# Order of the high and the low weight matmuls inside one product of a transformer layer's two projections

## The chip, the cores and the metric

The kernel runs on one core of one Trainium2 chip. The metric is the device time of one execution in microseconds (us). The same kernel was run three times; its median stands for it. A profile belongs to one further execution, whose own time is given beside it.

## The reference

The reference computes one decoder layer in float32 for a single sequence of 512 tokens with 2048 features. A first projection maps the input to 12288 columns: three groups of 1024 for a gated convolution, and queries, keys and values of three attention patterns of eight heads each. The convolution and the windowed attention follow, then an output projection, a residual and a layer norm. A second projection (up) maps to 2 x 5632 columns; a causal convolution of width 3, a gate and a down projection follow, and a second residual and layer norm. Cut to what matters here:

```
proj = x @ w_in                                # first projection: 512 x 2048 by 2048 x 12288
u, gate_b, gate_c, q, k, v = split(proj)
y_conv = gate_b * causal_conv3(gate_c * u, conv_w)
y_attn = dilated_window_attention(q, k, v, rel_bias)
x = layernorm(ALPHA * x + concat(y_conv, y_attn) @ w_out)
up = causal_conv3(x @ w_up, ffn_conv_w) + b    # second projection: 512 x 2048 by 2048 x 11264
a, g = split(up)
out = layernorm(ALPHA * x + (silu(g) * a) @ w_down)
```

## The kernel before, in words

**Splitting into high and low.** TensorE is used in a one-pass float32 form (`fp32r`) that keeps fewer bits of its operands. So every operand is split in two: a high part, rounded by a copy on ACT (L217 for weights, L312 for activations), and a low part, the rest, by a subtraction on DVE (L220 and L313). A product is then high x high + high x low + low x high. In the code `op.hi` and `op.lo` are the two parts of a weight block, `xh` and `xl` those of an activation block.

**Seven products instead of eight.** The two projections go by a scheme of Strassen's kind. The tokens, the features and the output columns are each halved. One output pair `p` (two blocks of 128 columns) is made of seven products of sums and differences of blocks instead of eight plain ones. `PROD` (L67) names for each product its activation block, its weight block and the region of PSUM in which it adds up; `MAIN` and `LAST` (L72, L73) are the orders in which the seven are run. A few pairs at the start of each projection are made otherwise: one by plain products (`PLAIN`), and five whose first two products are run ahead (`run_pre`, L378), while the activations still arrive. The first projection has 48 pairs, the second 44.

**One product.** A product sums over 1024 features, that is over eight steps `k` of 128. The weights are the stationary operand, a 128x128 block for each step, which is loaded anew for every matmul (the rows PEld of the profile). There are two forms of it.

- *Wide* (`product_wide`, L342). In each step a matmul with the high weights streams both parts of the activations side by side, 512 columns (L349), and a matmul with the low weights streams the high activations alone, 256 columns, into the second half of the same PSUM bank (L351). The two halves are added afterwards. That is 16 matmuls a product. `run_wide` (L414) uses it, for all regular pairs of the first projection and every third one of the second.
- *Narrow* (`product`, L362). In each step there are three matmuls of 256 columns into half a bank: high weights on high activations (L371), high weights on low activations (L372), low weights on high activations (L373). That is 24 matmuls a product. It is used for the pairs at the start of both projections and for two of three regular pairs of the second.

**What sets the order.** Each engine runs its instructions in the order in which the code issues them; the order is written out by hand (`manual_schedule`). `take` (L245) hands the next weight block over, after its low part has been issued on DVE; `free` (L254) gives its slot back and pumps further blocks: load by DMA on SP's queue (L182), the difference of two blocks on DVE where the scheme needs one (L207), high part on ACT, low part on DVE. There are four slots for high and four for low weights (`RING`, L60) and three for raw ones. After a product come the copies of its PSUM region (L446 for wide, L467 for narrow) and, some products later, the sums on DVE.

**The rest.** Attention (L767 to L872) is run with the output projection between its steps. The output and the down projection use a third form, `tm_unit` (L508 to L516): activations as the stationary operand, weights as the moving one, always 512 columns.

Of the kernel before, what the change touches and what calls it, by code (L numbers as in the profile page):

```python
# [18 lines left out]
P = 128  # L19
# [61 lines left out]
def _banks(q):  # L81
    return {"m" if PROD[i][2] in ("x1", "x2") else "n" for i in (q if isinstance(q, str) else [q])}
# [38 lines left out]
def layer_kernel(ctx: ExitStack, tc: tile.TileContext, xT, x, w_in, w_out, w_up, w_down, cw, fw, lnp, lnc, table,  # L121
# [3 lines left out]
    mm = nc.tensor.matmul  # L125
# [119 lines left out]
    def take():  # L245
        i = st["used"]
        if st["front"] <= i:
            pump()
        assert st["front"] > i
        back_upto(i + 1)  # L250
        st["used"] += 1
        return ops[i]
# [83 lines left out]
    def wide_region(p, name):  # L336
        rg = pairb.setdefault(p, {})
        if name not in rg:
            rg[name + "i"], rg[name] = get_bank()
        return rg[name]  # L340

    def product_wide(p, q, X, last):  # L342
        op = take()
        xn, _, reg = PROD[q]
        first = reg not in pairb.get(p, {})
        ps = wide_region(p, reg)
        for k in range(8):
            w = slice(k * P, (k + 1) * P)
            mm(ps, op.hi[:, w], X[xn].both(k), start=first and k == 0, stop=False,  # L349
               skip_group_check=True)  # L350
            mm(ps[:, 256:], op.lo[:, w], X[xn][0][:, k], start=False, stop=last and k == 7, skip_group_check=True)  # L351
        return op

    def region(p, name):
        rg = pairb.setdefault(p, {})
        b = "m" if name in ("x1", "x2") else "n"
        if b not in rg:
            rg[b + "i"], rg[b] = get_bank()
        return rg[b][:, 256:] if name in ("x1", "x3") else rg[b][:, :256]


    def product(p, q, X, last):  # L362
        op = take()
        for q in q if isinstance(q, str) else [q]:
            xn, _, reg = PROD[q]
            xh, xl = X[xn][0], X[xn][1]
            first = not _banks(q) & set(pairb.get(p, {}))
            ps = region(p, reg)
            for k in range(8):
                w = slice(k * P, (k + 1) * P)  # L370
                mm(ps, op.hi[:, w], xh[:, k], start=first and k == 0, stop=False, skip_group_check=True)  # L371
                mm(ps, op.hi[:, w], xl[:, k], start=False, stop=False, skip_group_check=True)  # L372
                mm(ps, op.lo[:, w], xh[:, k], start=False, stop=last and k == 7, skip_group_check=True)  # L373
        return op

# [2 lines left out]
    def run_pre(pl, X, keep, hook):  # L378
        pre = [(p, q) for p, seq, early in pl if early for q in seq]
        for i, (p, q) in enumerate(pre):  # L380
            free(product(p, q, X, False))
            if i == len(pre) - 4:
                for r in sorted({p for p, q in pre if q == "a"}):
                    kept[r] = keep()
                    for j, reg in enumerate(("x2", "x3")):
                        nc.scalar.activation(kept[r][:, j], region(r, reg), AF.Copy)
            hook()

    def run_plain(pl, X, otile, done, hook):
        def finish(p):  # L390
            o = otile()
            for i, reg in ((0, "x2"), (2, "x3")):
                nc.scalar.activation(o[:, i], region(p, reg), AF.Copy)
            for i, j, reg in ((1, 0, "x4"), (3, 1, "x1")):
                nc.vector.tensor_add(o[:, i], region(p, reg), kept[p][:, j])
            free_banks.extend((pairb[p]["ni"], pairb[p]["mi"]))
            del pairb[p]
            done(p, o)

        for p, seq, pre in pl:  # L400
            if pre or not _plain(seq):
                continue
            for i, q in enumerate(seq):
                op = product(p, q, X, not _banks(q) & set().union(*map(_banks, seq[i + 1:])))
                if i == len(seq) - 1:
                    later(2, functools.partial(finish, p))
                free(op)
                tick()
                hook()
# [4 lines left out]
    def run_wide(p, seq, X, stile, otile, put_block, done, hook):  # L414
# [26 lines left out]
        for i, q in enumerate(seq):  # L441
            left = set(seq[i + 1:])
            op = product_wide(p, q, X, PROD[q][2] not in {PROD[j][2] for j in left})
            if q in (1, 5, 6):
                sn[q] = stile(str(q))
                nc.scalar.activation(sn[q], pairb[p][PROD[q][2]], AF.Copy)  # L446
            for block, need in WNEED.items():
                if block not in sent and not need & left:
                    sent.add(block)
                    later(2, functools.partial(combine, block))  # L450
            free(op)
            tick()
            if hook:
                hook(p, q)

    def run_pairs(pl, X, stile, otile, bands, done, hook=None, put_block=None, every=1):
        for p, seq, pre in pl:
# [26 lines left out]
            for i, q in enumerate(seq):  # L484
                left = set(seq[i + 1:])
                op = product(p, q, X, not _banks(q) & set().union(*map(_banks, left)))
                if q in SNAP:
                    snap(q)
                for b, need in (("m", {7, 2, 5}), ("n", {3, 4, 6, 7})):
                    if b not in sent and not need & left:  # L490
                        sent.add(b)
                        later(2, functools.partial(combine, p, b, sn, box))
                free(op)
                tick()
                if hook:
                    hook(p, q)
# [70 lines left out]
    def xtile(pool, n):  # L567
        return Wide(pool.tile([P, 8, 2, 256], F32R, tag=n, name=nm(n)))
# [5 lines left out]
    X = {n: xtile(xp, n) for n in ("A11", "A12", "S1")}  # L574
# [489 lines left out]
    X = {n: xtile(xrp, n) for n in ("A22", "S1")}  # L1064
# [245 lines left out]
```

## Time and profile before

| | |
|---|---|
| median of three runs | 2632.48 us |
| lowest, highest | 2631.31, 2634.93 us |
| the profiled execution's own time | 2634.48 us |
| its span, first to last instruction | 2632.7 us |
| first projection | about 7 to 974 us of the span |
| attention and output projection | about 974 to 1245 us |
| second projection | about 1245 to 2140 us |
| down projection and second layer norm | about 2140 us to the end |

The profile shows one execution. PE is TensorE's matmuls, PEld its weight loads, DVE, ACT and POOL the other engines, SP the engine that issues most DMAs. A row of the groups gives the line, engine, operation, tiles (out<-in), shapes and count, then the busy time in us, the mean duration of one in ns, and the idle time of the engine just before these instructions with what ended it. A row of a stretch gives its bounds and length, then for each engine the busy time with the number of instructions in parentheses, and at the end the granted TensorE clock, the share of the DMA engines and GB/s. A row of the timeline gives start and duration in us, engine, line, operation, tiles and shapes. The recorded duration of a matmul reaches from its start to the end of its pass through the array, and the next one begins before that end.

### The profile page before, as it was taken

To read this page: it belongs to the slowest core of one execution; us is meant where nothing else is said; L and a number is where in the kernel's file an instruction comes from. 1 tells how busy PE (TensorE), PEld (TensorE's weight loads), DVE (VectorE), ACT (ScalarE), POOL (GpSimd) and SP (SyncE) were. 2 spreads that over 40 slices of the span, in tenths; PEclk is the share of its full clock that TensorE was granted. 3 is DMA by queue.
4 is the path that set the end of the run, shared out by engine and by line. 5 is a ranking of instruction groups with operands and counts; after the bars stand their busy time and mean duration, and the time that the engine had idled before them with its cause. 6 is when DMAs were issued, how large, how long until landed. Compare 5 with 4: busy or idle time off the path is not lost.

```text
span 2632.7 us, 39148 instructions
## 1 busy us (share of the span) xinstructions
PE 2595.9 (99%) x16034; PEld 2323.1 (88%) x16034; DVE 2157.0 (82%) x2575; ACT 1211.6 (46%) x1617; POOL 125.7 (5%) x217
## 2 busy tenths in 40 slices
PE   9999999999999989999999999999999999999997
PEld 8988888888888878888999999999999988888886
DVE  7989888888888877657899999999998966765557
ACT  5544444444444444434655555555555553222220
POOL 0000100000000002220000000000000000000000
PEclk9999999999999999999999999999999999999999
DMA  7422543333333357653543333333333353434331
GB/s 243 169 102 108 182 148 129 132 138 132 128 140 133 125 208 257 220 184 105 184 148 125 118 119 112 121 122 116 123 118 119 125 204 140 152 124 160 112 128 64
DMA packets 70229, 376.34 MB, mean 143 GB/s; under 512 B 9921, under 2 KB 13793, under 8 KB 35361
## 3 DMA queue, kind: packets, MB, share of 16 engines
q1 hardware_dynamic: 51680, 311.47, 33.6%
q0 software_dynamic: 18368, 62.36, 6.5%
q8 instruction: 126, 2.06, 0.3%
q14 instruction: 55, 0.44, 0.1%
HBM read 328.61 MB, written 48.84 MB: 143 GB/s over the span
## 4 chain that ended last, share of the span: by engine, by line
PE 90%; DVE 5%; DMA 2%; ACT 2%; issue 1%; SPq 0%; POOL 0%; DVEq 0%; ACTq 0%
PE bk L349 27%; PE bk L351 13%; PE bk L514 8%; PE bk L516 8%; PE bk L515 8%; PE bk L371 8%; PE bk L372 8%; PE bk L373 8%; DVE wlo L220 1%; DVE tt L207 1%; DMA raw<-in_w_in_dram 1%; DMA ycr<-yc_d 1%; PE bk L848 1%; ACT whi L217 1%; PE bk L794 0%
## 5 line engine op out<-in xcount | busy, mean ns | idle before, releaser
L217 ACT ACTIVATE whi<-raw 128x1024 fp32r<-128x1024 f32 x394 | 414.5, 1057 | 586.5 <-PE bk L516 210.4
L349 PE MATMUL bk<-S,whi 128*128 128x512 f32 x1760 | 624.4, 399 | 1.4 <-ACT s L446 1.4
L220 DVE TENSOR_TENSOR wlo<-raw,whi 128x1024 fp32r<-128x1024 f32 x394 | 480.0, 1221 | 151.3 <-ACT whi L217 149.8
L217 ACT ACTIVATE whi<-tt 128x1024 fp32r<-128x1024 f32 x360 | 381.2, 1059 | 364.2 <-PE bk L349 157.4
L351 PE MATMUL bk<-S,wlo 128*128 128x256 f32 x1760 | 494.1, 281 | 0.0
L349 PE MATMUL bk<-A,whi 128*128 128x512 f32 x1320 | 469.9, 399 | 0.0
L220 DVE TENSOR_TENSOR wlo<-tt,whi 128x1024 fp32r<-128x1024 f32 x360 | 439.4, 1221 | 33.7 <-ACT whi L217 30.1
L349 PEld LDWEIGHTS bk<-S,whi 128*128 128x128 f32 x1760 | 330.7, 188 | 84.5 <-ACT s L446 2.1
L351 PE MATMUL bk<-A,wlo 128*128 128x256 f32 x1320 | 370.7, 281 | 0.0
L351 PEld LDWEIGHTS bk<-S,wlo 128*128 128x128 f32 x1760 | 332.4, 189 | 0.0
L371 PE MATMUL bk<-S,whi 128*128 128x256 f32 x1152 | 326.5, 283 | 1.8 <-ACT sm L467 0.9
L372 PE MATMUL bk<-S,whi 128*128 128x256 f32 x1152 | 326.0, 283 | 0.0
L373 PE MATMUL bk<-S,wlo 128*128 128x256 f32 x1152 | 326.0, 283 | 0.0
L349 PEld LDWEIGHTS bk<-A,whi 128*128 128x128 f32 x1320 | 248.1, 188 | 62.4 <-issue 1.5
L371 PE MATMUL bk<-A,whi 128*128 128x256 f32 x936 | 265.9, 284 | 2.2 <-ACT A L312 1.2
L373 PE MATMUL bk<-A,wlo 128*128 128x256 f32 x936 | 265.3, 283 | 2.6 <-DVE wlo L220 2.6
L372 PE MATMUL bk<-A,whi 128*128 128x256 f32 x936 | 265.0, 283 | 0.9 <-DVE A L313 0.9
L351 PEld LDWEIGHTS bk<-A,wlo 128*128 128x128 f32 x1320 | 249.4, 189 | 0.0
L371 PEld LDWEIGHTS bk<-S,whi 128*128 128x128 f32 x1152 | 221.1, 192 | 2.8 <-ACT z L467 1.7
L372 PEld LDWEIGHTS bk<-S,whi 128*128 128x128 f32 x1152 | 221.1, 192 | 0.0
L373 PEld LDWEIGHTS bk<-S,wlo 128*128 128x128 f32 x1152 | 221.1, 192 | 0.0
L207 DVE TENSOR_TENSOR tt<-raw,tt 128x1024 f32<-128x1024 f32 x180 | 219.1, 1217 | 0.0
(206 smaller groups left out, 4154.0 us busy)
## 6 DMA issues: line engine op xcount, KB each, us to landing
raw<-in_w_in_dram SPq DMA_DIRECT2D x97, 1024.0 KB, 4.9
raw<-in_w_up_dram SPq DMA_DIRECT2D x89, 1024.0 KB, 5.3
raw<-in_w_down_dram SPq DMA_DIRECT2D x44, 1024.0 KB, 4.9
qkv_d<-o POOLq DMA_DIRECT2D x36, 512.0 KB, 3.8
raw<-in_w_out_dram SPq DMA_DIRECT2D x16, 1024.0 KB, 7.3
act_d<-z POOLq DMA_DIRECT2D x44, 256.0 KB, 5.1
qk<-qkv_d SPq DMA_DIRECT2D x7, 1536.0 KB, 10.3
ar<-act_d SPq DMA_DIRECT2D x9, 1024.0 KB, 7.0
```

What stands on the lines that cost most here:

```text
L207: nc.vector.tensor_sub(self.src, v[0], prev)
L217: nc.scalar.activation(self.hi, self.src, AF.Copy)
L220: nc.vector.tensor_sub(self.lo, self.src, self.hi.bitcast(F32))
L349: mm(ps, op.hi[:, w], X[xn].both(k), start=first and k == 0, stop=False, skip_group_check=True)
L351: mm(ps[:, 256:], op.lo[:, w], X[xn][0][:, k], start=False, stop=last and k == 7, skip_group_check=True)
L371: mm(ps, op.hi[:, w], xh[:, k], start=first and k == 0, stop=False, skip_group_check=True)
L372: mm(ps, op.hi[:, w], xl[:, k], start=False, stop=False, skip_group_check=True)
L373: mm(ps, op.lo[:, w], xh[:, k], start=False, stop=last and k == 7, skip_group_check=True)
L514: mm(banks[n], yh[:, tt], op.hi[:, w], start=first and i == 0, stop=False)
L515: mm(banks[n], yh[:, tt], op.lo[:, w], start=False, stop=False)
L516: mm(banks[n], yl[:, tt], op.hi[:, w], start=False, stop=last and i == 1)
L848: nc.tensor.transpose(ps[:, i * P:(i + 1) * P], src[:, n, s:s + P], ident)
```

## The change

Within one product, all matmuls with the high weights are issued first, for the eight steps `k` in turn, and then all matmuls with the low weights. This is done in the wide form and in the narrow one. In the narrow form the high weights' two matmuls of a step stay together. The first matmul of a product still starts the sum in its PSUM bank, and the last one (low weights, `k == 7`) still closes it. Nothing else is touched: neither the order of the products, nor the loads, the splitting or the copies.

```diff
@@ product_wide @@
         for k in range(8):
             w = slice(k * P, (k + 1) * P)
-            mm(ps, op.hi[:, w], X[xn].both(k), start=first and k == 0, stop=False,
-               skip_group_check=True)
+            mm(ps, op.hi[:, w], X[xn].both(k), start=first and k == 0, stop=False, skip_group_check=True)
+        for k in range(8):
+            w = slice(k * P, (k + 1) * P)
             mm(ps[:, 256:], op.lo[:, w], X[xn][0][:, k], start=False, stop=last and k == 7, skip_group_check=True)
         return op
@@ product @@
                 mm(ps, op.hi[:, w], xh[:, k], start=first and k == 0, stop=False, skip_group_check=True)
                 mm(ps, op.hi[:, w], xl[:, k], start=False, stop=False, skip_group_check=True)
+            for k in range(8):
+                w = slice(k * P, (k + 1) * P)
                 mm(ps, op.lo[:, w], xh[:, k], start=False, stop=last and k == 7, skip_group_check=True)
         return op
```

## The prediction, made before the changed kernel was run

> **What bounds the kernel now.** I read the page first: its busy lines, the chain that ended last, then the costliest groups. The rows are
>
> ```profile
> span 2632.7 us, 39148 instructions
> PE 2595.9 (99%) x16034; PEld 2323.1 (88%) x16034; DVE 2157.0 (82%) x2575; ACT 1211.6 (46%) x1617; POOL 125.7 (5%) x217
> PEclk9999999999999999999999999999999999999999
> PE 90%; DVE 5%; DMA 2%; ACT 2%; issue 1%; SPq 0%; POOL 0%; DVEq 0%; ACTq 0%
> PE bk L349 27%; PE bk L351 13%; PE bk L514 8%; PE bk L516 8%; PE bk L515 8%; PE bk L371 8%; PE bk L372 8%; PE bk L373 8%; DVE wlo L220 1%; DVE tt L207 1%; DMA raw<-in_w_in_dram 1%; DMA ycr<-yc_d 1%; PE bk L848 1%; ACT whi L217 1%; PE bk L794 0%
> L349 PE MATMUL bk<-S,whi 128*128 128x512 f32 x1760 | 624.4, 399 | 1.4 <-ACT s L446 1.4
> L349 PE MATMUL bk<-A,whi 128*128 128x512 f32 x1320 | 469.9, 399 | 0.0
> L351 PEld LDWEIGHTS bk<-S,wlo 128*128 128x128 f32 x1760 | 332.4, 189 | 0.0
> L371 PE MATMUL bk<-S,whi 128*128 128x256 f32 x1152 | 326.5, 283 | 1.8 <-ACT sm L467 0.9 <-ACT z L467 0.8
> ```
>
> TensorE is busy 99% of the span, and 90% of the chain is TensorE. The two lines of the wide product alone hold 40% of it: L349 (high weights, 512 columns) and L351 (low weights, 256 columns). L349 ran 1760 + 1320 = 3080 times, so there are 3080 high-low pairs in 385 wide products of eight pairs. The three lines of the narrow product hold 24%. The duration of one matmul is not its price: 399 ns is recorded for one L349, but the next begins long before that ends. The price is the spacing from start to start. So the second view is what TensorE waited for at all, and the third the timeline.
>
> ```profile
> PE bk L514 <- ACT yc L312: 7.6, 1, 7.6
> ...
> PE bk L373 <- DVE wlo L220: 2.6, 4, 0.8
> ...
> PE bk L349 <- ACT s L446: 1.4, 2, 0.7
> ```
>
> The columns are total us, times, longest. In the wide products TensorE lost 1.4 us to waits of every kind. In the narrow ones, low weights that came late cost 2.6 us, four times. So the change can't win by hiding a wait. Only the spacing within a product is left, and there I look at single matmuls:
>
> ```profile
> 499.27 0.40 PE L349 MATMUL bk<-A,whi 128*128 128x512 f32 x1
> ...
> 500.33 0.40 PE L349 MATMUL bk<-A,whi 128*128 128x512 f32 x1
> 500.57 0.28 PE L351 MATMUL bk<-A,wlo 128*128 128x256 f32 x1
> 500.68 0.40 PE L349 MATMUL bk<-A,whi 128*128 128x512 f32 x1
> 500.91 0.28 PE L351 MATMUL bk<-A,wlo 128*128 128x256 f32 x1
> 501.03 0.40 PE L349 MATMUL bk<-A,whi 128*128 128x512 f32 x1
> 501.27 0.28 PE L351 MATMUL bk<-A,wlo 128*128 128x256 f32 x1
> ...
> 502.09 0.40 PE L349 MATMUL bk<-S,whi 128*128 128x512 f32 x1
> ```
>
> One product begins at 499.27 and the next (other operand, S) at 502.09: eight pairs in 2.82 us. From a high to the following low it is 0.24, 0.23 and 0.24 us, mean 237 ns; from a low to the next high 0.11 and 0.12 us. Now the same price from a long stretch of wide products, beside one in which only 256-column matmuls run (narrow products) and one in which only 512-column matmuls run (the down projection, L514 to L516), each with a weight load of its own:
>
> ```profile
> 500.00:900.00 400.00, 400.00 (x1134) 212.73 (x1133) 1.00 0.37 132
> ...
> 73.00:139.00 66.00, 66.00 (x552) 66.00 (x552) 62.50 (x62) 32.20 (x45) 0.69 (x1) 1.00 0.42 150
> ...
> 2200.00:2400.00 200.00, 200.00 (x884) 165.59 (x883) 137.66 (x168) 48.77 (x47) 6.47 (x12) 1.00 0.39 146
> ```
>
> The first row counts L349 alone, the other two all of TensorE. A count includes the instruction that was already under way when the stretch began, so I take one off. A pair in the wide product costs 400 / 1133 = 353.0 ns. A 256-column matmul among its like costs 66 / 551 = 119.8 ns, a 512-column one among its like 200 / 883 = 226.5 ns. Side by side the two make 346.3 ns. **Alternating them costs 6.7 ns a pair more than running each kind by itself.** That is the whole opening for this change.
>
> The same program shows that alternation need not cost this. For a short stretch it doesn't:
>
> ```profile
> 301.00 0.39 PE L349 MATMUL bk<-A,whi 128*128 128x512 f32 x1
> ...
> 303.77 0.39 PE L349 MATMUL bk<-S,whi 128*128 128x512 f32 x1
> ```
>
> Eight pairs in 2.77 us are 346.3 ns. So 353.0 is one rhythm into which the alternation falls, and 346.3 another. Why it falls into the slower one for most of the time no row tells; I only use that the homogeneous stretches keep 119.8 and 226.5.
>
> **The change part by part.** No instruction is added or removed: as many matmuls, weight loads, ACT and DVE operations and DMAs. Only the order on TensorE changes, within one product.
>
> *Wide products.* Before: eight times high, low. After: eight highs, then eight lows. Seven of the eight highs are followed by a high and seven lows by a low, for which I take 226.5 and 119.8. 3080 pairs x 6.7 ns = 20.6 us less. All of it lies on the path, since TensorE waits for nothing there. What is left of alternation are two switches a product, one at its middle and one at its end, where there were sixteen. If the excess belongs to the switches, each costs 6.7 / 2 = 3.35 ns, and 385 products x 2 keep 2.6 us of it. Between 0 and 2.6 I take 1.3: **-19.3 us**.
>
> Does the weight load become the bound in a run of eight short matmuls? The load is recorded with 189 ns, longer than the 119.8. But the stretch 73 to 139 is nothing but short matmuls with such loads (552 and 552), and its spacing is 119.8. Loads overlap, and the low run is bounded by that row.
>
> The Trainium skill, "TensorE: Matmul & The Clock Gate", section "Back-to-back issue gap", speaks against this change: it gives the gap of a warm matmul as N / 2.4 + 2.5 ns, a function of the column count alone. By it a pair would cost about 216 + 109 = 325 ns in either order, and the sum for the wide products would be zero. The trace doesn't agree: 353.0 and 346.3 for the same pair in one program, at a granted clock of 1.00 in all the rows above.
>
> *Narrow products.* Before: high on the high part of X, high on the low part, low on the high part. After: sixteen highs, then eight lows. All three are 256 columns with an own load at 119.8 already, so the steady cost is nothing.
>
> *Waits.* The first low matmul of a product waits for the low weights (DVE, L220). It moves behind eight 512-column highs (8 x 226.5 = 1.81 us) or sixteen short ones (16 x 119.8 = 1.92 us). Behind it only the other lows are queued, and on other engines only what the product's end releases anyway. The 2.6 us of that wait, all of it near the start, should go. Against it: a product whose X arrives in pieces now runs all its lows after the last piece. It happens once near the start:
>
> ```profile
> 34.37 1.29 DVE L313 TENSOR_TENSOR A<-S,A 128x512 fp32r<-128x512 f32 x2 [1.04 <-ACT A L312]
> ...
> 35.12 0.38 PE L372 MATMUL bk<-A,whi 128*128 128x256 f32 x1 [0.34 <-DVE A L313]
> ...
> 36.53 0.28 PE L371 MATMUL bk<-A,whi 128*128 128x256 f32 x1
> ```
>
> The last piece is there at 34.37 + 1.29 = 35.66. Before, the product ends at 36.53, when the next begins. After, three highs still need the last piece (0.36) and eight lows follow (0.96): 35.66 + 0.36 + 0.96 = 36.98, or 0.45 us later. Of the 2.6 us, then, up to 2.15 remain, or nothing, if these first products wait for their DMAs instead. I take **-1 us**.
>
> *Buffers.* The high weights' slot comes free eight lows earlier (0.96 us), the low weights' slot and X at the product's end as before. ACT may start its next conversion earlier; nobody waits for it in these stages.
>
> *Does the feeding keep up?* The busiest feeder is DVE:
>
> ```profile
> 500.00:900.00 400.00, 400.00 (x2267) 346.99 (x2266) 351.82 (x384) 192.71 (x224) 14.32 (x20) 1.00 0.37 132
> ...
> 1398.00:2120.00 722.00, 722.00 (x5382) 690.39 (x5381) 663.61 (x724) 389.33 (x505) 19.52 (x36) 1.00 0.35 119
> ```
>
> In the first projection it is busy 351.82 of 400 us; with TensorE 6.7 / 353.0 = 1.9% quicker that is 351.82 / 392.4 = 90%. In the second projection it is busy 663.61 of 722 us, 92%, but there only one block in three is wide, and the share rises to 92.5%. Four weight slots lie between them. I cost it at nothing; without that cover the second projection's share of the gain, at most a quarter, is lost.
>
> The 7.6 us wait after the first projection hangs on a DMA issued from that stage, so it moves along.
>
> Sum: -19.3 - 1 = **-20.3 us**. The profiled execution took 2634.48 us (span 2632.7), 2.0 above the median of the runs, 2632.48. Its own time becomes 2614.2, the median 2612.2; I say **2612**. Within this case 2607 to 2617: the switches (0 to 2.6), the start (+0.5 to -2.2), and one or two ns on the two spacings.
>
> **The rivals.**
>
> 1. *The high run keeps its spacing (slower).* The 237 ns from a high to the next matmul could belong to the wide high matmul itself and its operands, and the short low after it could be what makes up for it. Then the high run goes at 237, the low run at 119.8, and a pair costs 356.8: 3080 x 3.8 = 11.7 us more, 2644. It decides from 233.2 ns on (353.0 - 119.8). For it: the 237 in the rows is measured at this very line. Against it: the 226.5 of the down projection has the same columns, the same 128x128 load and likewise adds up in one bank. Chance 0.08.
>
> 2. *Order does not matter (no change).* The excess may sit in each matmul of the wide product, or in a rhythm into which the new order falls as well. Then the sum is zero but for the start: 2631, between 2628 and 2636. For it: most of the wide stages keep to 353.0, whatever DVE and ACT do beside them. Against it: the stretch at 301, with the same lines at 346.3. The skill's gap rule above would end here too. Chance 0.11.
>
> 3. *Part of the gain.* The high run settles between 226.5 and 233.2, or DVE takes the second projection's share back. Half of the gain is about 2622, between 2617 and 2628. For it: the DVE share of 92%; against it: almost no wait of TensorE today. Chance 0.11.
>
> **How the numbers follow.** The forecast has 0.70. What a measurement of this kernel can tell from no change is about 0.2%, 5.3 us. Faster by more than that: the forecast and nearly all of the third rival, 0.80. Within it: the second and the rest, 0.12. Slower: the first, 0.08. The range takes in the forecast's own 2607 to 2617, one more ns in either spacing below it, and most of the third rival above: 2605 to 2626.
>
> **What would show each step.** In the changed profile, a stretch of wide products such as 500 to 880 must hold a high matmul every 346 to 347 ns instead of 353; inside a product the timeline must show highs 226 to 227 ns apart and lows 119 to 120. The narrow stretch must keep 119.8. The wait of narrow low matmuls for DVE must go from 2.6 us to almost nothing, and TensorE must gain no new wait in either projection. The prediction is wrong if the highs stay above 230 ns, if the lows go above 123, or if the spacings are as I say and TensorE then waits for DVE.

## The result, and the profile after

| | before | changed |
|---|---|---|
| median, the profiled run among them | 2632.84 us (4 runs) | 2618.77 us (4 runs) |
| lowest, highest | 2631.31, 2634.93 us | 2617.22, 2619.59 us |
| the profiled execution's own time | 2634.48 us | 2619.59 us |
| its span | 2632.7 us | 2617.8 us |

The changed kernel takes 0.9945 of the time before, 95% interval 0.9928 to 0.9963: 14.1 us less by the medians, 14.9 us by the two profiled executions. The prediction was 20.3 us less. The direction was right, and so was the place of the gain; the saving is about a third smaller than forecast. The range, 2605 to 2626, holds the result, but the median lies just outside the forecast's own 2607 to 2617 and inside the 2617 to 2628 of the third rival, part of the gain. The lines of the code have moved by a few: the wide product's high matmul is still L349, its low one is now L352, the narrow ones are L372, L373 and L376.

From the page of the changed kernel, the rows that answer to those of before:

```profile
span 2617.8 us, 39148 instructions
PE 2586.3 (99%) x16034; PEld 2329.8 (89%) x16034; DVE 2156.1 (82%) x2575; ACT 1205.6 (46%) x1617; POOL 125.4 (5%) x217
PE 92%; DVE 4%; DMA 2%; ACT 1%; issue 1%; SPq 0%; POOL 0%; DVEq 0%; ACTq 0%
...
L349 PE MATMUL bk<-S,whi 128*128 128x512 f32 x1760 | 440.9, 392 | 0.0
```

The counts are the same as before, and TensorE still carries the chain. The busy time of L349 on S has fallen from 624.4 to 440.9 us, which is far more than anything that was gained. That fall is none: the recorded durations of neighbouring matmuls overlap, and a row counts an overlap within its own group once. Highs used to overlap lows and now overlap highs. Only starts can be compared.

The two stages with wide products, from the first wide matmul to the start of the projection's last matmul, first of the kernel before, then of the changed one (bounds and length in us, then busy time and count of PE, PEld, DVE, ACT and POOL):

```profile
139.17:974.03 834.86, 833.43 (x4711) 720.59 (x4710) 738.09 (x812) 401.61 (x465) 34.82 (x51) 1.00 0.39 137
1378.99:2140.10 761.11, 761.11 (x5658) 726.98 (x5656) 698.54 (x763) 411.71 (x533) 22.23 (x41) 1.00 0.35 122
```

```profile
139.76:963.74 823.98, 823.98 (x4711) 723.15 (x4710) 737.08 (x813) 398.79 (x466) 34.74 (x51) 1.00 0.40 140
1367.11:2125.18 758.07, 758.07 (x5657) 727.58 (x5656) 699.35 (x763) 409.91 (x534) 22.15 (x41) 1.00 0.36 123
```

The first projection's wide stage is 10.88 us shorter, the second projection's 3.04 us: 13.9 of the 14.9 us. The start is 0.6 us longer (139.76 against 139.17). What lies between the two stages is 1.6 us shorter (403.37 against 404.96); in the profiles of the runs below this stretch took 395.5 to 407.1 us, so I give it no cause. The end is equal, 492.6 us in both.

Now the price of a product. Kernel before, 132 products after the one that begins at 499.27 (a row of the prediction):

```profile
872.39 0.40 PE L349 MATMUL bk<-A,whi 128*128 128x512 f32 x1
...
499.28:872.38 373.10, 373.10 (x1057) 198.41 (x1057) 1.00 0.37 134
```

and the changed kernel, also over 132 products:

```profile
511.34 0.86 PE L349 MATMUL bk<-A,whi 128*128 128x512 f32 x3
...
880.06 1.32 PE L349 MATMUL bk<-A,whi 128*128 128x512 f32 x5
...
511.35:880.05 368.70, 264.41 (x1056) 189.91 (x1057) 1.00 0.38 134
```

The last row of each counts the highs between the two starts, eight a product (one of the 1057 had begun before). A wide product fell from 373.12 / 132 = 2826.7 ns to 368.72 / 132 = 2793.3 ns. 385 products x 33.4 ns = 12.9 us. The two spacings of the prediction would have made it 8 x 346.3 = 2770 ns. Where the rest stays is seen inside one product of the changed kernel; equal matmuls in a row are merged, and the third row is that of a later window, in which only the last three highs appear:

```profile
611.90 2.00 PE L349 MATMUL bk<-A,whi 128*128 128x512 f32 x8
...
613.06 0.84 PE L349 MATMUL bk<-A,whi 128*128 128x512 f32 x3
613.74 1.11 PE L352 MATMUL bk<-A,wlo 128*128 128x256 f32 x8
614.70 0.40 PE L349 MATMUL bk<-S,whi 128*128 128x512 f32 x1
```

The last three highs take 613.74 - 613.06 = 0.68 us, 227 ns each, as in the down projection. The eight lows take 0.96 us, 120 ns each, as in a narrow product. But the first five highs take 613.06 - 611.90 = 1.16 us, 232 ns each. By the starts in the trace the eight highs are 234, 236, 228, 232, 231, 227, 227 and 227 ns apart, on average over the products from 300 to 960 us, and the first low is followed after 113 ns instead of 120. **A run of highs that follows lows needs five matmuls until it reaches its own spacing.** The narrow matmuls between 73 and 139 us kept theirs, 120 ns.

Last, TensorE's waits in the changed kernel, in the first projection's start and over the whole span; from 139 to 960 us no wait is left:

```profile
PE bk L517 <- ACT yc L312: 6.5, 1, 6.5
PE bk L372 <- ACT A L312: 2.6, 2, 1.5
...
PE bk L373 <- DVE A L313: 1.5, 2, 0.9
...
PE bk L372 <- ACT whi L217: 1.2, 1, 1.2
```

The waits for low weights (2.6 us) and for the copy L446 (1.4 us) are gone. At the start, the waits for the pieces of X have grown in their place (2.6 + 1.5 us, where 1.2 + 0.9 us stood before).

### The profile page after: what moved, and what is told of

Same layout as the page of the kernel before. It is cut to its first block, busy times and chain, and to the rows that moved or that the text cites. A ratio compares the mean times of both kernels' runs of the same rounds, so it can differ in the third digit from the quotient of the medians.

```text
span 2617.8 us, 39148 instructions
## 1 busy us (share of the span) xinstructions
PE 2586.3 (99%) x16034; PEld 2329.8 (89%) x16034; DVE 2156.1 (82%) x2575; ACT 1205.6 (46%) x1617; POOL 125.4 (5%) x217
## 4 chain that ended last, share of the span: by engine, by line
PE 92%; DVE 4%; DMA 2%; ACT 1%; issue 1%; SPq 0%; POOL 0%; DVEq 0%; ACTq 0%
PE bk L349 27%; PE bk L352 14%; PE bk L376 8%; PE bk L373 8%; PE bk L372 8%; PE bk L517 8%; PE bk L519 8%; PE bk L518 8%; DVE wlo L220 1%; DMA raw<-in_w_in_dram 1%; DVE tt L207 1%; DMA ycr<-yc_d 1%; PE bk L851 1%; PE bk L797 0%; PE bk L781 0%
## 5 line engine op out<-in xcount | busy, mean ns | idle before, releaser
L217 ACT ACTIVATE whi<-raw 128x1024 fp32r<-128x1024 f32 x394 | 413.9, 1057 | 521.2 <-PE bk L519 204.1
L217 ACT ACTIVATE whi<-tt 128x1024 fp32r<-128x1024 f32 x360 | 380.6, 1057 | 292.4 <-DVE tt L207 167.6
L349 PE MATMUL bk<-S,whi 128*128 128x512 f32 x1760 | 440.9, 392 | 0.0
L349 PEld LDWEIGHTS bk<-S,whi 128*128 128x128 f32 x1760 | 316.5, 189 | 56.9 <-ACT s L449 0.4
L349 PE MATMUL bk<-A,whi 128*128 128x512 f32 x1320 | 330.8, 392 | 0.0
L372 PE MATMUL bk<-S,whi 128*128 128x256 f32 x1152 | 283.1, 283 | 0.8 <-ACT z L470 0.8
L373 PE MATMUL bk<-S,whi 128*128 128x256 f32 x1152 | 282.7, 283 | 0.0
L349 PEld LDWEIGHTS bk<-A,whi 128*128 128x128 f32 x1320 | 237.4, 189 | 44.0 <-ACT whi L217 0.9
L352 PEld LDWEIGHTS bk<-S,wlo 128*128 128x128 f32 x1760 | 240.1, 190 | 17.1
L352 PE MATMUL bk<-S,wlo 128*128 128x256 f32 x1760 | 245.4, 282 | 0.0
L372 PE MATMUL bk<-A,whi 128*128 128x256 f32 x936 | 233.5, 286 | 4.0 <-ACT A L312 2.6
L373 PE MATMUL bk<-A,whi 128*128 128x256 f32 x936 | 232.9, 286 | 1.6 <-DVE A L313 1.5
L372 PEld LDWEIGHTS bk<-S,whi 128*128 128x128 f32 x1152 | 221.1, 192 | 1.7 <-ACT z L470 1.7
L373 PEld LDWEIGHTS bk<-S,whi 128*128 128x128 f32 x1152 | 221.2, 192 | 0.0
L352 PEld LDWEIGHTS bk<-A,wlo 128*128 128x128 f32 x1320 | 180.1, 190 | 12.9
L517 PE MATMUL bk<-whi,A 128*128 128x512 f32 x480 | 186.7, 389 | 0.0
L518 PE MATMUL bk<-wlo,A 128*128 128x512 f32 x480 | 186.7, 389 | 0.0
L519 PE MATMUL bk<-whi,A 128*128 128x512 f32 x480 | 186.7, 389 | 0.0
L372 PEld LDWEIGHTS bk<-A,whi 128*128 128x128 f32 x936 | 181.6, 194 | 5.3 <-ACT A L312 3.1
```

The lines of the kernel that those rows point to most:

```text
L217: nc.scalar.activation(self.hi, self.src, AF.Copy)
L517: mm(banks[n], yh[:, tt], op.hi[:, w], start=first and i == 0, stop=False)
L518: mm(banks[n], yh[:, tt], op.lo[:, w], start=False, stop=False)
L519: mm(banks[n], yl[:, tt], op.hi[:, w], start=False, stop=last and i == 1)
```

## The experiments

State of the theories before the first run. **S (settling):** the gain comes from runs of equal width, and what it lacks comes from the change from 256 to 512 columns, after which some highs are slow. **P (place):** the slow highs belong to the beginning of a product (new weights, another PSUM bank), whatever the widths. **N:** part of the gain came from the narrow products. **R:** any mixture falls back into the slow rhythm of before.

### Highs first in the wide products alone

```diff
 def product_wide: as in the change
 def product:      as in the kernel before
```

> Highs first in the wide products alone; the narrow ones stay as before. Theory S (settling): a change of matmul width costs time once, at the switch from lows (256 columns) to highs (512 columns), because the first five highs are 233, 236, 228, 233 and 231 ns apart before they reach 227; then a wide product lasts 2793 ns here as in the changed kernel, and the first wide product begins at 139.2 us as in the kernel before, so the time is about 2618 us. Rival N: part of the 14 us came from the narrow products; then this run is slower than the changed kernel by that part.

Measured: 2621.05 us, 0.9956 of the kernel before (0.9941 to 0.9971), the same as the changed kernel within the intervals. Its two stages with wide products last 824.0 and 758.1 us, as in the changed kernel, so the gain is in them.

### Highs first in the narrow products alone

```diff
 def product_wide: as in the kernel before
 def product:      as in the change
```

> Highs first in the narrow products alone. Both theories: wide products stay at 2827 ns. The lows are all behind the last piece of X at the start, so I expect the first wide product at 139.8 instead of 139.2 us, and the time within 1.5 us of the kernel before. Rival N: it is faster by 1 us or more, because the four waits for low weights are gone.

Measured: 2631.02 us against 2631.21, ratio 1.000 (0.999 to 1.001). The interval alone, 2.6 us to either side, couldn't exclude the 1 us of N. The profile says more: the second projection's stage, in which two of three regular pairs are narrow, takes 761.11 us as in the kernel before, and the first wide product begins at 139.13 us, against 139.17. So that half of the change does nothing that can be measured, although the waits for low weights are gone from its profile too. The expected 0.6 us at the start didn't come either.

### Four highs, four lows, twice a product

```diff
+        for k0 in (0, 4):
+            for k in range(k0, k0 + 4):   # highs
+            for k in range(k0, k0 + 4):   # lows
```

> Wide products as four highs, four lows, four highs, four lows; narrow ones as before. Settling: two switches a product, each with four slow highs (23 ns in all) and one quick low (6.5 ns): 2773 + 33 = 2806 ns a product. Rival P (the excess belongs to the beginning of a product: new weights, another PSUM bank): the second group of highs is not slow, 2793 ns. Rival R (any mixture falls back into the slow rhythm): 2827 ns.

Measured: 2622.34 us in one run. The starts of two products that lie 132 apart, and the groups within one product:

```profile
495.81 0.86 PE L350 MATMUL bk<-A,whi 128*128 128x512 f32 x3
...
866.29 0.63 PE L350 MATMUL bk<-A,whi 128*128 128x512 f32 x2
...
610.89 1.09 PE L350 MATMUL bk<-A,whi 128*128 128x512 f32 x4
611.82 0.63 PE L353 MATMUL bk<-A,wlo 128*128 128x256 f32 x4
612.29 1.09 PE L350 MATMUL bk<-A,whi 128*128 128x512 f32 x4
613.22 0.64 PE L353 MATMUL bk<-A,wlo 128*128 128x256 f32 x4
613.70 1.09 PE L350 MATMUL bk<-A,whi 128*128 128x512 f32 x4
```

370.48 / 132 = 2806.7 ns a product, where S gave 2806. The second group of highs, in the middle of the product with the same weights and the same bank, is as slow as the first: 0.93 us for four, 232 ns each, in both. P is out for this kernel, and so is R.

### Two highs, two lows, four times a product

```diff
+        for k0 in (0, 2, 4, 6):
+            for k in range(k0, k0 + 2):   # highs
+            for k in range(k0, k0 + 2):   # lows
```

> Wide products as two highs, two lows, four times over. Settling: four switches, each with two slow highs (6.3 + 9.3 ns) and one quick low (6.5 ns): 2773 + 36 = 2809 ns a product. Rival P (beginning of a product): 2793 ns or less. Rival R (slow rhythm): 2827 ns.

Measured: 2617.47 us in one run.

```profile
494.57 0.62 PE L350 MATMUL bk<-A,whi 128*128 128x512 f32 x2
...
862.41 0.63 PE L350 MATMUL bk<-A,whi 128*128 128x512 f32 x2
...
611.38 0.39 PE L353 MATMUL bk<-A,wlo 128*128 128x256 f32 x2
611.61 0.62 PE L350 MATMUL bk<-A,whi 128*128 128x512 f32 x2
612.07 0.40 PE L353 MATMUL bk<-A,wlo 128*128 128x256 f32 x2
612.31 0.63 PE L350 MATMUL bk<-A,whi 128*128 128x512 f32 x2
```

367.84 / 132 = 2786.7 ns a product. S gave 2809. P's "2793 ns or less" holds as a number, but not as a mechanism: the highs are slow in every group, also in the middle of a product, as S says (0.46 us for two; 233 ns each on average over the trace). What S lacked are the two lows behind them, 0.23 us, 115 ns each on average: they win back part of it. So S in the form "each switch costs a fixed sum" has fallen. What stands is that highs behind lows are slow and that lows behind few highs are quick; how the two balance must be measured for each pattern.

### Lows of 512 columns too

```diff
-            mm(ps[:, 256:], op.lo[:, w], X[xn][0][:, k], ...)
+            mm(ps, op.lo[:, w], X[xn].both(k), ...)
```

> Wide products alone changed: eight highs, then eight lows that stream 512 columns as well (both parts of X, into the whole bank), so low weights on the low part of X are computed too, which the kernel leaves out otherwise. No matmul of a product differs in width from its neighbours. Theory S (the excess comes with a change of width): every spacing is 226.7 ns from the first high on, 16 x 226.7 = 3627 ns a product. Rival P (beginning of a product: new weights, another bank): the first five highs still go at 233, 236, 228, 233, 231, so 3647 to 3655 ns. Either way far slower as a whole, about 2940 us.

Measured: 2932.07 us. One run of highs from its beginning, behind a product's lows of the same width:

```profile
613.43 1.98 PE L349 MATMUL bk<-S,whi 128*128 128x512 f32 x8
615.25 0.62 PE L352 MATMUL bk<-S,wlo 128*128 128x512 f32 x2
```

1.82 us for eight, 227.5 ns each, with no slow ones at the beginning. Five slow highs would make it 1.84, so the mean over a hundred products and a product that follows narrow matmuls are needed beside it:

```profile
139.49 2.00 PE L349 MATMUL bk<-A,whi 128*128 128x512 f32 x8
141.33 1.98 PE L352 MATMUL bk<-A,wlo 128*128 128x512 f32 x8
...
976.10 0.62 PE L349 MATMUL bk<-A,whi 128*128 128x512 f32 x2
```

A hundred products from 613.43 on end at 976.10: 3626.7 ns each, sixteen times 226.7. The first wide product of all stands right behind 256-column matmuls, and its highs take 1.84 us: by the starts in the trace they are 233, 236, 228, 233 and 231 ns apart, then 227. All 14 products of this run that follow narrow matmuls last 3654 or 3655 ns, 28 more than the others that nothing interrupts. Weights, bank and product change at every product here, as in the changed kernel; the slow highs come only where 256-column matmuls stand before them. (With the width goes the part of the bank that is written; these runs don't part the two.) With this P is out altogether, and the rival of the prediction that gave the 237 ns to the high matmul itself is out too: the same line with the same operands keeps 227.

### The highs of two products, then the lows of both

```diff
-            op = product_wide(p, q, X, ...)
+            # twos: 1 and 5, 6 and 3, 7 and 4; product 2 alone
+            if q not in high:
+                for j in (q, two.get(q)): high[j] = wide_high(p, j, X)    # eight highs each
+            wide_low(p, q, X, ..., high[q])                               # eight lows
```

> Wide products in twos: the highs of both, then the lows of both (six of the seven products of a pair of columns; the seventh alone); narrow products as before. Theory S: only the first product of each two has slow highs and only its first low is quick, 20 ns for two products where the changed kernel has 40; 2783 ns a product in the twos, 2793 for the seventh, 60 ns x 55 = 3.3 us less than the changed kernel, about 2615 us. Rival P: both products begin slowly, 2793 ns each and about 2618 us.

Measured: 2631.09 us, 1.000 of the kernel before (0.9993 to 1.001). The products themselves did what S said, from the starts of two that lie 132 apart:

```profile
495.28 0.63 PE L349 MATMUL bk<-A,whi 128*128 128x512 f32 x2
...
862.90 0.63 PE L349 MATMUL bk<-A,whi 128*128 128x512 f32 x2
```

367.62 / 132 = 2785.0 ns, where six of seven at 2783 and one at 2793 make 2784.4. But it is lost again, and neither time that was expected came. Most of the loss is in the second projection, whose wide stage took 770.62 us against 758.07 in the changed kernel:

```profile
1363.45:2134.07 770.62, 761.20 (x5657) 726.67 (x5656) 697.42 (x764) 410.38 (x536) 22.15 (x41) 1.00 0.35 120
...
PE bk L349 <- ACT z L457: 9.4, 13, 0.7
...
PE bk L349 <- ACT s L457: 3.0, 2, 1.6
```

There TensorE waits 13 times, once for each wide pair of columns, for a copy of PSUM (L457): product 6 adds into the bank of product 1 and now begins only eight lows behind it. That distance alone doesn't make the wait: the 42 wide pairs of the first projection have the same order, and TensorE waits there only twice (3.0 us).

### The two products together, in another order; and that order alone

```diff
-    seqs: MAIN (1, 5, 6, 3, 7, 4, 2) for the wide pairs
+    seqs: LAST (1, 5, 2, 6, 3, 7, 4) for the wide pairs
-    two = {1: 5, 6: 3, 7: 4}
+    two = {1: 5, 2: 6, 3: 7}
```

> Wide products in twos as in the run before, but all wide pairs of columns take the order 1, 5, 2, 6, 3, 7, 4, in twos 1 5, 2 6, 3 7 and 4 alone, so that 16 highs or 8 highs of another product lie between a product's lows and the next high into the same PSUM bank. If the twos lost their gain because the next highs followed the copy of that bank too closely, the waits for L457 (12.4 us) go and the time is 3 us under the changed kernel, about 2615 us. If they lost it otherwise (weights that come too late because two are in use at once), it stays near 2631.

> Highs first in each wide product by itself, with the order 1, 5, 2, 6, 3, 7, 4 for all wide pairs of columns, narrow products as before. Both theories: 2793 ns a wide product and about the changed kernel's time, 2618 us within 2 us, so that the twos can be told from the order.

Measured: the twos 2665.47 us, 1.013 of the kernel before (1.0115 to 1.0146); the order alone 2620.80 us, 0.9964 (0.9951 to 0.9976), like the changed kernel. The order alone is 0.8 us above the band that was expected for it; its stages with wide products, 823.9 and 758.6 us, are those of the changed kernel within 0.5 us. So the order does no harm by itself, and with the twos it costs 45 us more. Neither time that was expected for the twos came, 2615 or near 2631, and my theory of the waits has fallen:

```profile
PE bk L376 <- ACT z L478: 15.0, 15, 1.2
PE bk L349 <- ACT s L457: 12.4, 28, 2.5
...
PE bk L378 <- DVE wlo L220: 2.5, 4, 0.8
```

The waits for copies didn't go; they grew. Those for L457 are 12.4 us again, now 28 of them where there were 15, and the narrow matmuls behind the wide pairs wait 15.0 us for L478, where it was 0.8. The weight loads wait for the same copies, in the first projection (first row) and in the second (second row):

```profile
PEld bk L349 <- ACT s L457: 28.6, 39, 3.0
...
PEld bk L376 <- ACT z L478: 17.6, 14, 1.4
```

That covers what the stages are longer than with the order alone: 849.3 against 823.9 us, and 774.7 against 758.6. So the time went into waits for copies. Why the copies come late is argued, not shown: two products in use at once leave two of the four weight slots for what comes next, and the copies stand on ACT in line with the weight conversions. No run has more slots.

### The groups of two and the changed kernel, timed side by side

> The groups of two again, timed. The spacings repeat themselves from run to run in the kernel before, so I expect 2786.6 ns a wide product again, 6.7 ns x 385 = 2.6 us under the changed kernel in these stages, and 1.4 us of waits for the copies of PSUM that the changed kernel doesn't have: about 2617 us. If the rhythm depends on how a run starts, the product's time will differ from 2786.6.

> The changed kernel again, beside the two others on the same chip: 2793.3 ns a wide product, about 2618.5 us.

Measured: groups of two 2617.57 us, 0.9951 (0.9937 to 0.9965); the changed kernel 2619.47 us, 0.9958 (0.9946 to 0.9971). The groups of two are the quickest version in these runs, by 1.9 us of medians, though their intervals overlap. By the profiles of these two runs a wide product takes 2786.7 and 2793.3 ns, as expected: 6.6 ns, 2.5 us in all. The groups of two have the 1.4 us of waits that the changed kernel is rid of, and so their two stages are 1.0 us shorter together (823.6 and 757.5 us against 824.0 and 758.1). The rest of the 1.9 us comes from outside these stages and has no cause that I know.

## Why the prediction was right or wrong

**The opening was real.** Equal matmuls in a row keep 227 and 120 ns inside the wide product, as the two homogeneous stretches of before had it, and DVE keeps up (737.08 of 823.98 us, 89.5%, where 90% was forecast; 699.35 of 758.07, 92%, in the second projection). Two rivals are out: the highs didn't keep 237, and the sum is not zero. The third is out in the half that named DVE, for which no wide product of the changed kernel waits. Its other half came near: the eight highs settle at 227 ns, but on average they are 230 ns apart (1.84 us), and the time lies in its band. The pair came to 349.2 ns, where the prediction asked for 346 to 347. The gap rule of the Trainium skill ("TensorE: Matmul & The Clock Gate", "Back-to-back issue gap") that was weighed there, which that section gives for an isolated matmul, has no place for the order. These runs don't agree with it: one pair in the same operands cost 353.3, 350.8, 349.2 or 348.3 ns (2826.7, 2806.7, 2793.3 and 2786.7 over eight), by order alone.

**The term that was mis-sized is that of the two switches left in each product.** I set it at 0 to 2.6 us and took 1.3, by sharing the excess of 6.7 ns a pair evenly among sixteen switches. It measured 385 x (2793.3 - 2773.3) = 7.7 us, of an opening that was 385 x (2826.7 - 2773.3) = 20.6 us, as forecast. (2773.3 is eight pairs of 120.0 and 226.7 ns. The prediction's 119.8 and 226.5 are a little short: by the trace 550 and 882 matmuls start in the two stretches, one fewer than were counted. A matmul of 256 columns is recorded with 283 ns and the next starts after 120, so more than one was already under way.)

The even sharing was the error. In the alternation of before, a slow high (236 ns on average) is followed at once by a low that wins something back (117 ns); behind a run of eight lows, five slow highs stand in a row (232 against 227 ns) and only a little is won back afterwards. Above 2773 ns, a product keeps 53 ns with sixteen switches, 13 with eight (groups of two), 33 with four (groups of four) and 20 with two: the excess isn't even monotonic in the number of switches.

The kernel before shows the price of each of the two switches once, and the prediction didn't look there. At 2140.22 us the 512-column matmuls of the down projection begin behind narrow ones, and at 1245.18 us narrow ones begin behind 512-column ones:

```profile
2140.22 0.40 PE L514 MATMUL bk<-whi,A 128*128 128x512 f32 x1
...
2141.38 0.39 PE L516 MATMUL bk<-whi,A 128*128 128x512 f32 x1
...
2142.51 0.39 PE L515 MATMUL bk<-wlo,A 128*128 128x512 f32 x1
...
1245.18 0.28 PE L371 MATMUL bk<-A,whi 128*128 128x256 f32 x1
1245.29 0.28 PE L372 MATMUL bk<-A,whi 128*128 128x256 f32 x1
```

The first five matmuls take 1.16 us, 232 ns each, the next five 1.13, 226 each; the first narrow one is followed after 0.11 us. By the starts in the trace the five are 233, 236, 229, 232 and 231 ns apart, 28 ns in all above 226.7, and the narrow switch wins back 7. So 21 ns a product, 8 us in all, could have been read beforehand, and with it the forecast would have been about 14 us less instead of 20.

**The step "Buffers" was costed at nothing and gave 1.4 us.** The high weights' slot comes free eight lows earlier, and I wrote that nobody waits for it. Twice in the first projection somebody did, at one remove: TensorE waited 1.4 us for the copy L446. The chain of the kernel before leads there from the end of a high matmul:

```profile
178.56 0.24 PE bk L349
178.88 1.06 ACT whi L217
...
187.47 0.58 ACT s L446
188.10 0.50 PE bk L349
```

A high matmul gives a weight slot back, the conversion L217 begins, and sums, conversions and parts of the convolution on ACT and DVE follow one another until the copy. In the changed kernel the chain of this stretch is TensorE alone. The wait goes with the moment at which the last high is done. It is 1.4 us before and in the groups of two (which end with two lows), 1.6 with the narrow products alone changed, 0.8 in the groups of four, and none in the four profiles with eight highs and then eight lows in each wide product. These kernels fit it; nothing else was varied to test it.

**The start was set at -1 us and came out at +0.6 in the profiled run.** The waits for low weights did go, and in spite of the longer waits for X TensorE's waits up to 139 us add up to 6.6 us, where they were 7.5. But one thing more lies in these microseconds. Here is the same stretch in the kernel before and in the changed one, which is the second row:

```profile
32.50:39.30 6.80, 5.28 (x43) 4.88 (x42) 5.04 (x7) 4.87 (x7) 0.00 (x0) 1.00 0.91 308
```

```profile
32.50:39.30 6.80, 5.60 (x24) 4.97 (x23) 5.33 (x7) 4.87 (x7) 0.00 (x0) 0.50 0.91 312
```

The granted clock fell to 0.50 for 6.8 us, and TensorE issued 24 matmuls where it had issued 43. The Trainium skill, "TensorE: Matmul & The Clock Gate", section "What's actually happening", says that the gate looks at activity in a free-running window of 3413 ns; the 6.8 us agree with two of them. Whether the change makes such drops likelier stays open: between 30 and 45 us all three profiles with the narrow products changed have one (3.4 us in the other two), and of the nine with those of before two have one, of 3.4 us. The start as a whole shows no gain and no loss: the first wide product begins at 139.1 to 139.8 us in the three, and at 138.3 to 139.9 us in the nine.

In sum: -12.9 (spacing) - 1.4 (copies) + 0.6 (start) - 1.6 (the stretch between, which varies) and + 0.4 (seven wide products of before went in the quick rhythm already, 54 ns less than the others) make the -14.9 of the profiled executions. The 1.4 and the 1.6 us were no part of the forecast: that the result lies as near to it as it does is in part luck.

## What to carry to other kernels

On a kernel that TensorE bounds, the price of a matmul is its spacing to the next start, and that depends on its neighbours: compare a mixed stretch with homogeneous stretches of the same shapes in the same trace before any experiment. A difference found in this way was an upper bound of what sorting gave here, since the places where runs of the two shapes meet cost something of their own. Look for one such place in the trace and read its price, matmul by matmul, instead of sharing the excess out; here the start of the down projection held it. Sorting further, over two products, was eaten up by waits for the copies of PSUM, so the reach of a reorder is set by what stands around it.

## What the runs showed of the hardware that I had not expected

- The spacing has a memory of several matmuls. With a load for every matmul, 512 columns settle at 227 ns and 256 at 120 ns, but after a change from 256 to 512 it takes five matmuls (233, 236, 228, 233 and 231 ns), at a granted clock of 1.00 and with no wait in the trace. What it is that settles, these runs don't tell.
- The same alternation has two rhythms: a quick one, 346.7 ns a pair, and a slow one, in which products of 2819, 2830 and 2831 ns take turns, 353 ns a pair. The quick one lasted for seven products in the kernel before and for some two dozen with the narrow products alone changed. The orders in groups of two, four and eight within a product each kept to one product time (within 1 ns, but for the few products that something else interrupts).
- The recorded busy time of a group of matmuls can fall by 30% (624.4 to 440.9 us) through nothing but the order.
